# Output projection and two feed-forward pairs read their tokens woven from both halves of the sequence

## The chip, the cores and the metric

The kernel runs on one core of a Trainium2 chip. The metric is the device time of one execution in microseconds; lower is better. A core has a matrix engine (TensorE, PE in the profile), which multiplies a stationary operand of 128x128 (loaded by a separate instruction, PEld) with a moving operand of up to 512 columns and accumulates the product in a bank of PSUM; a vector engine (VectorE, DVE), a scalar engine (ScalarE, ACT) and GpSimd (POOL) for elementwise work; and DMA queues, here those of SyncE (SP) and GpSimd.

## The reference, cut to what matters

One decoder block over 512 tokens, float32, with a model width of 1024 and a feed-forward width of 2816:

```python
h = rmsnorm(x, norm1_g)
proj = h @ w_in                      # short convolution, attention and merge gates
...
mix = gm[..., :D_MODEL] * (y_a @ w_a_out) + gm[..., D_MODEL:] * (y_b @ w_b_out)
x = x + mix @ w_o                    # the output projection
h = rmsnorm(x, norm2_g)
gu = h @ w_ffn_in
g = causal_dwconv(gu[..., :D_FF], ffn_conv_w) + ffn_conv_b
x = x + (silu(g) * gu[..., D_FF:]) @ w_ffn_out
```

## The kernel before, in words

Everything is kept transposed: channels lie on the 128 partitions and the 512 tokens along the free dimension. A float32 product is made of three products in the chip's `float32r` type: each operand is split into a high part (a rounded copy, names ending in `h`) and a low part (the rest, names ending in `l`), and `dense` issues, for each block of 128 inputs, high weight by high x (L158), high weight by low x (L161) and low weight by high x (L163, or L165 where the low weights come in a loop of their own after the others, `lo_last`). The matmuls of one call accumulate in one PSUM region, `acc`.

The stages follow one another on TensorE: input projections, attention, convolution and gates, the output projection, the feed-forward part. A scheduler that simulates the program orders the instructions of each engine; `behind` adds a few orders by hand.

The output projection runs over eight tiles of 128 output channels, in the order 0, 4, 1, 5, 2, 6, 3, 7 (`n` counts the place, `j` the tile). Each loads its weights (`load_w`), takes a bank of 512 columns (tile `po_j`), multiplies the 8 input blocks of `mix_h` and `mix_l` with all 512 tokens, and is added to x by VectorE (L1091). Then `x_forms` makes from it what the feed-forward part multiplies: sums and differences of halves, split again into `xf_h` and `xf_l`, whose last dimension is half the sequence, TH = 256 tokens.

The feed-forward input product goes over pairs of channel tiles, f = 0, 2, ..., 20, each with n = 0 (the convolved gate) and n = 1 (the up part). `ff_pair` makes one n of a pair by Strassen's scheme (in Winograd's form): seven products instead of eight, each by `product`, which accumulates 4 blocks of 128 inputs over 256 columns of half a bank (tile `p`). VectorE combines the halves of the banks (`sums`), and ScalarE copies the first of them (`p1`). The down products (tile `pdn`) of earlier pairs are placed among them by `share`.

Three lines elsewhere are used in the prediction for what they show. L738 and L766 are score products of the attention whose moving operand `kk` is read in two runs; L817 adds a product to an accumulator that it walks as two runs of 128 columns, 256 columns apart (`a4[:, :, b]`). L555 and L566 belong to the compressed keys: L555 multiplies by a row read at every second element, and L566 subtracts operands read at every eighth and every fourth element and writes every fourth. L319 and L199 are plain elementwise lines over contiguous elements.

Of the kernel before, what the change touches and what calls it, by code (L numbers as in the profile page):

```python
# [18 lines left out]
P = 128  # L19
D = 1024  # L20
S = 512
KD = D // P
# [46 lines left out]
HOLD_PT = 4  # L69
HOLD_PO = 6  # L70
A22_BY_DMA = ((0,0),(0,1),)
N_DOWN = 4
N_LAG = 1
INV_FREQ = (10000.0 ** (-np.arange(HALF) / HALF)).astype(np.float32)
# [21 lines left out]
def tile_block(ctx: ExitStack, tc: tile.TileContext, xT, pos, par, par2, w_tok, w_a3, w_gate, w_ao, w_bo, w_o,  # L96
# [12 lines left out]
    def const(shape, name, dt=F32, pool=sb):  # L109
        return pool.tile(shape, dt, name=name, tag=name)  # L110
# [27 lines left out]
    def d_bank(name):  # L138
        return bank("d", name, 2)

    def s_bank(name):
        return bank("s", name, 3)

    def t_bank(name):
        return bank("t", name, 2)

    def o_bank(name):
        return bank("o", name, 1)


    loads, splits = [], []

    def dense(acc, units, first=True, last=True, held={}, lo_last=False):


        n = len(units)
        for i, (wh, wl, xh, xl) in enumerate(units):
            m = nc.tensor.matmul(acc, wh, xh, start=first and i == 0, stop=False)  # L158
            if i in held:
                behind(m, held[i])  # L160
            nc.tensor.matmul(acc, wh, xl, start=False, stop=False)  # L161
            if not lo_last:
                m = nc.tensor.matmul(acc, wl, xh, start=False, stop=last and i == n - 1)  # L163
        for i, (wh, wl, xh, xl) in enumerate(units if lo_last else ()):
            m = nc.tensor.matmul(acc, wl, xh, start=False, stop=last and i == n - 1)  # L165
        return m
# [169 lines left out]
    def behind(later, earlier):  # L336

        tc.add_manual_dep(later.ins, earlier.ins.name,
                          mybir.DependencyInfo(mybir.DependencyClass.NoSync, mybir.DependencyReason.DATA),
                          reason="order")  # L340
# [196 lines left out]
    def w_units(w, xh, xl, nk, k0=0, koff=0):  # L537
        wh, wl = w
        return [(wh[:, (koff + k) * P:(koff + k + 1) * P], wl[:, (koff + k) * P:(koff + k + 1) * P],
                 xh[:, k0 + k, :], xl[:, k0 + k, :]) for k in range(nk)]  # L540
# [453 lines left out]
    def form_a22(f, n, raw, form):  # L994
        h, l = (pw.tile([P, half], F32R, name=f"t{x}{n}_{f}", tag=f"t{x}", bufs=1) for x in "hl")
        if (f, n) in A22_BY_DMA:
            nc.scalar.activation(l, raw[:, half:D], AF.Copy, scale=-1.0)
# [30 lines left out]
    mix_h = const([P, KD, S], "mix_h", F32R, pc)  # L1028
    mix_l = const([P, KD, S], "mix_l", F32R, pc)
    for i in range(4):  # L1030
# [6 lines left out]
        w = load_w(w_bo[i], D, f"bo{i}", after=(ends["pc"], ends["pl"]) if i == 0 else ())  # L1037
        for n, j in enumerate((2 * i, 2 * i + 1)):
            acc = t_bank(f"pmb{j}")
            dense(acc, w_units(w, yb_h, yb_l, 4, koff=4 * n), held={0: gate} if j == 0 else {})  # L1040
            m = tb[j]
# [14 lines left out]
    xf_h = const([P, 4, 7, TH], "xf_h", F32R, px)  # L1056
    xf_l = const([P, 4, 7, TH], "xf_l", F32R, px)
# [5 lines left out]
    def x_forms(j):  # L1063

        k = j % 4
        if j < 4:
            xv[k] = pv.tile([P, 6, TH], F32, name=f"xv{k}", tag="xv", bufs=2)

        v = xv[k]
        o = v[:, 2 * (j // 4):2 * (j // 4) + 2].rearrange("p a t -> p (a t)")  # L1070
        nc.scalar.activation(o, x1[:, j, :], AF.Copy, scale=par_sb[:, G2 + j:G2 + j + 1])
        put = lambda b, a: split(xf_h[:, k, b], xf_l[:, k, b], v[:, a])
        if j < 4:
            nc.vector.tensor_sub(v[:, 4], v[:, 1], v[:, 0])
            put(slice(B11, T1 + 1), slice(0, 5, 4))
        else:
            nc.vector.tensor_sub(v[:, 5], v[:, 3], v[:, 1])
            put(slice(B21, B22 + 1), slice(2, 4))
            nc.vector.tensor_sub(v[:, 0], v[:, 3], v[:, 4])
            nc.vector.tensor_sub(v[:, 1], v[:, 2], v[:, 0])  # L1080
            put(T3, 5)
            put(slice(T2, T4 + 1), slice(0, 2))

    order = [k + 4 * i for k in range(4) for i in range(2)]
    for n, j in enumerate(order):
        w = load_w(w_o[j], D, f"o{j}")
        nc.sync.dma_start(x1[:, j, :], xT[:, j, :])
        acc = d_bank(f"po_{j}")
        dense(acc, w_units(w, mix_h, mix_l, KD), lo_last=True)
        xj = x1[:, j, :]  # L1090
        nc.vector.tensor_add(xj, xj, acc)  # L1091
        x_forms(j)
        sq = sq2 if n == 0 else pc.tile([P, S], F32, name=f"sqb{j}", tag="tb", bufs=3)
        nc.scalar.activation(sq, xj, AF.Square)
        if n > 0:
            nc.vector.tensor_add(sq2, sq2, sq)
# [25 lines left out]
    def ff_pair(f, n, c, form, held=None):  # L1122
        nm = f"{n}_{f}"
        b1, b26 = s_bank(f"p1{nm}"), t_bank(f"p26{nm}")
        b37, b45 = s_bank(f"p37{nm}"), o_bank(f"p45{nm}")
        lo, hi = slice(0, TH), slice(TH, S)

        def product(acc, wf, x, k0=0, k1=4, held={}):
            wh, wl = form[wf]
            dense(acc, [(wh[:, k * P:(k + 1) * P], wl[:, k * P:(k + 1) * P], xf_h[:, k, x], xf_l[:, k, x])  # L1130
                        for k in range(k0, k1)], first=k0 == 0, last=k1 == 4, held=held, lo_last=True)

        def sums(dst, bank, v):

            nc.vector.tensor_tensor(dst, bank.rearrange("p (a t) -> p a t", a=2), v[:, None, :].to_broadcast([P, 2, TH]),
                                    op=ALU.add)

        p1 = pw.tile([P, TH], F32, name=f"p1{nm}", tag="p1", bufs=2)
        c1, c2 = c[:, :, 0:TH], c[:, :, TH:]
        product(b1[:, lo], "a11", B11)  # L1140
        m = nc.scalar.activation(p1, b1[:, lo], AF.Copy)
        if (f, n) == (N_DOWN, 1):
            behind(m, ends["sh"])
        if held:

            product(b45[:, hi], 1, T1)
            product(b26[:, lo], "a12", B21, 0, 3)
            product(b37[:, hi], 3, T3, 0, 3)
            product(b26[:, lo], "a12", B21, 3, 4)
            product(b26[:, hi], 2, T2, held={0: held[0]})  # L1150
            product(b37[:, hi], 3, T3, 3, 4, held={0: held[1]})
        else:
            product(b26[:, lo], "a12", B21)
            product(b26[:, hi], 2, T2)
            product(b37[:, hi], 3, T3)
        sums(c1, b26, p1)
        product(b37[:, lo], 4, B22)
        sums(c2, b37, c1[:, 1])
        if not held:
            product(b45[:, hi], 1, T1)  # L1160
        product(b45[:, lo], "a22", T4)
        sums(c[:, 1].rearrange("p (a t) -> p a t", a=2), b45, c2[:, 1])
        nc.vector.tensor_add(c2[:, 0], c2[:, 0], b45[:, hi])
# [41 lines left out]
    def down_products(f0, n, j0, w, accs=(), last=False):  # L1205

        h, l = w
        per = D // (n * P)
        js = range(j0, j0 + per)
        for j in sorted(js, key=lambda j: last and j not in accs):  # L1210
            cols = [slice(((j - j0) * n + k) * P, ((j - j0) * n + k + 1) * P) for k in range(n)]
            held = j in accs
            for t, acc in accs[j] if held else ((slice(0, S), (d_bank if last or accs == () else t_bank)(f"pdn{j}_{f0}")),):
                acc = acc[:, t]
                dense(acc, [(h[:, c], l[:, c], *(v[:, t] for v in a_hl[f0 + k])) for k, c in enumerate(cols)],
                      first=not (held and last), last=not held or last, lo_last=not accs)
                if held and not last:
                    continue
                xj = x1[:, j, t]
                nc.vector.tensor_add(xj, xj, acc)  # L1220
                if last:
                    (nc.scalar if t.start else nc.sync).dma_start(out[j][:, t], xj)


    def quarter(q):
        return q // N_DOWN * N_DOWN, N_DOWN, D // P // N_DOWN * (q % N_DOWN)

    def share(f, n):
        q = f + n - N_DOWN - N_LAG
        if 0 <= q < NF - N_DOWN - 2:  # L1230
            down_products(*quarter(q), down_weights(*quarter(q), by_dma=True))

    for f in range(0, NF, 2):
# [4 lines left out]
            for j, bank_of in enumerate((d_bank, d_bank, s_bank, s_bank, s_bank, o_bank), 1)}  # L1238
    for n, f0 in ((N_DOWN, NF - N_DOWN - 2), (2, NF - 2)):
        for j in range(0, KD, D // (n * P)):  # L1240
# [66 lines left out]
```

## Time and profile before

| | |
|---|---|
| median of 3 runs | 716.74 us (716.40 to 717.13) |
| span of the profiled execution | 714.1 us |
| TensorE busy | 709.2 us, 99% of the span |
| weight loads busy | 635.9 us, 89% |
| VectorE busy | 573.9 us, 80% |
| ScalarE busy | 414.9 us, 58% |
| granted TensorE clock | 1.000 (mean) |

The span reaches from the first to the last instruction of one profiled execution. The time of that execution with what lies around its span is not recorded apart; the median of the runs is 2.6 us above the span. In the profile, a group of instructions has its line, engine, operation, tiles written and read, shapes and count, then the busy time in us and the mean duration of one in ns, then the idle time of the engine before them. A row of the timeline begins with its start in us and its length in us. A row for one line has the durations (least, median, most) in ns.

### The profile page before, as it was taken

The numbers are of one execution on the slowest core, as the hardware profiler recorded it, in microseconds if no ns is written. First come the engines' busy times: TensorE is split into PE (matmuls) and PEld (weight loads), VectorE is DVE, ScalarE is ACT, GpSimd is POOL, SyncE is SP. The second block draws the span as 40 slices with busy tenths as digits, with TensorE's granted clock in tenths as the row PEclk, the third lists the DMA queues.
The fourth block names the chain that finished last, engine by engine and source line by source line (L and its number), as shares of the span: only waits on it lengthen the run. The fifth ranks groups of instructions, "written<-read, shape, count | busy, mean of one in ns | idle before, by whom it ended". The sixth has DMA issues, their size and how long they took to land.

```text
span 714.1 us, 11190 instructions
## 1 busy us (share of the span) xinstructions
PE 709.2 (99%) x4275; PEld 635.9 (89%) x4275; DVE 573.9 (80%) x988; ACT 414.9 (58%) x706; POOL 124.6 (17%) x111
## 2 busy tenths in 40 slices
PE   9999999999999999999999999999999999999997
PEld 8999888888888888888889999999999999999986
DVE  7978978785566784788876999899898998989833
ACT  7776566777767875444665665555455554455320
POOL 1022443343333311232002011010000010000000
PEclk9999999999999999999999999999999999999999
DMA  8633552121111122246547466745655556552313
GB/s 306 219 86 105 156 127 71 49 90 59 60 60 59 60 63 86 90 146 199 184 133 163 117 149 173 181 119 133 167 144 130 137 127 158 129 148 89 118 30 118
DMA packets 36804, 88.19 MB, mean 124 GB/s; under 512 B 7440, under 2 KB 10896, under 8 KB 36752
## 3 DMA queue, kind: packets, MB, share of 16 engines
q1 hardware_dynamic: 30672, 74.42, 32.7%
q0 software_dynamic: 5648, 12.58, 10.7%
q8 instruction: 33, 0.54, 0.3%
q10 hardware_dynamic: 432, 0.49, 0.2%
q14 instruction: 19, 0.16, 0.1%
HBM read 85.39 MB, written 2.10 MB: 123 GB/s over the span
## 4 chain that ended last, share of the span: by engine, by line
PE 92%; issue 4%; DMA 2%; DVE 1%; POOL 0%; ACT 0%; POOLq 0%; SPq 0%; DVEq 0%
PE p L158 8%; PE p L165 8%; PE p L161 8%; PE pdn L161 4%; PE pdn L158 4%; PE pg L161 4%; PE pg L163 4%; PE pg L158 4%; PE pdn L165 4%; PE pa L158 3%; PE pa L161 3%; PE pt L805 2%; PE po L165 2%; PE po L158 2%; PE po L161 2%
## 5 line engine op out<-in xcount | busy, mean ns | idle before, releaser
L158 PE MATMUL p<-xf_h,sh 128*128 128x256 f32 x352 | 86.4, 280 | 0.0
L161 PE MATMUL p<-xf_l,sh 128*128 128x256 f32 x352 | 86.0, 278 | 0.0
L158 PEld LDWEIGHTS p<-xf_h,sh 128*128 128x128 f32 x352 | 66.5, 189 | 0.1
L161 PEld LDWEIGHTS p<-xf_l,sh 128*128 128x128 f32 x352 | 65.9, 187 | 0.0
L942 ACT ACTIVATE sh<-s 128x1024 fp32r<-128x1024 f32 x44 | 45.7, 1050 | 21.0 <-DVE s L987 17.8
L943 DVE TENSOR_TENSOR sl<-s,sh 128x1024 fp32r<-128x1024 f32 x44 | 53.1, 1215 | 2.8 <-ACT sh L942 2.8
L165 PE MATMUL p<-xf_h,sl 128*128 128x256 f32 x352 | 54.9, 279 | 0.0
L968 POOL DMA_DIRECT2D wl_d<-in_w_dn_dram x16 | 19.1, 1195 | 203.9 <-ACT wl_d L965 203.9
L161 PE MATMUL pdn<-al,wh_d 128*128 128x512 f32 x134 | 52.4, 391 | 0.0
L158 PE MATMUL pdn<-ah,wh_d 128*128 128x512 f32 x134 | 52.0, 390 | 0.0
L163 PE MATMUL pg<-xg_h,wl_g 128*128 128x512 f32 x128 | 50.5, 395 | 0.0
L161 PE MATMUL pg<-xg_l,wh_g 128*128 128x512 f32 x128 | 50.3, 393 | 0.0
L158 PE MATMUL pg<-xg_h,wh_g 128*128 128x512 f32 x128 | 50.3, 393 | 0.0
L165 PEld LDWEIGHTS p<-xf_h,sl 128*128 128x128 f32 x352 | 47.4, 188 | 0.3
L158 PE MATMUL p<-xf_h,wh_s 128*128 128x256 f32 x176 | 43.3, 280 | 0.0
L161 PE MATMUL p<-xf_l,wh_s 128*128 128x256 f32 x176 | 43.1, 278 | 0.0
L756 ACT ACTIVATE e<-sc,mx 128x512 f32<-128x512 f32 (+3 forms) x64 | 33.1, 520 | 16.5 <-DVE mx L755 14.7
L158 PE MATMUL pa<-xg_h,wh_a 128*128 128x512 f32 x96 | 37.9, 395 | 0.0
L161 PE MATMUL pa<-xg_l,wh_a 128*128 128x512 f32 x96 | 37.6, 392 | 0.0
L782 ACT ACTIVATE e<-e,sums 128x512 f32<-128x512 f32 (+3 forms) x64 | 30.7, 552 | 8.2 <-DVE sums L732 8.0
L809 DVE TENSOR_TENSOR pl<-pt,ph 128x512 fp32r<-128x512 f32 x40 | 27.2, 683 | 10.2 <-ACT ph L808 10.0
L165 PE MATMUL pdn<-ah,wl_d 128*128 128x512 f32 x128 | 34.2, 389 | 0.0
(361 smaller groups left out, 2108.9 us busy)
## 6 DMA issues: line engine op xcount, KB each, us to landing
wr_s<-in_w_ff_dram SPq DMA_DIRECT2D x44, 512.0 KB, 3.7
wr_d<-in_w_dn_dram SPq DMA_DIRECT2D x22, 512.0 KB, 3.7
wr_g<-in_w_gate_dram SPq DMA_DIRECT2D x16, 512.0 KB, 3.5
wl_d<-in_w_dn_dram POOLq DMA_DIRECT2D x16, 512.0 KB, 7.0
wr_a<-in_w_a_dram SPq DMA_DIRECT2D x12, 512.0 KB, 3.5
wr_t<-in_w_tok_dram SPq DMA_DIRECT2D x10, 524.0 KB, 5.3
wr_o<-in_w_o_dram SPq DMA_DIRECT2D x8, 512.0 KB, 3.5
wr_ao<-in_w_ao_dram SPq DMA_DIRECT2D x4, 512.0 KB, 3.4
```

What stands on the lines that cost most here:

```text
L158: m = nc.tensor.matmul(acc, wh, xh, start=first and i == 0, stop=False)
L161: nc.tensor.matmul(acc, wh, xl, start=False, stop=False)
L163: m = nc.tensor.matmul(acc, wl, xh, start=False, stop=last and i == n - 1)
L165: m = nc.tensor.matmul(acc, wl, xh, start=False, stop=last and i == n - 1)
L756: nc.scalar.activation(e[:, i, 0:nk], sc[:, o:o + nk], AF.Exp, bias=mx[:, i], accum_out=sums[:, i])
L782: nc.scalar.activation(v, v, AF.Copy, scale=sums[:, i])
L805: ends["pt"] = nc.tensor.transpose(pt[:, i * P:(i + 1) * P], e[:, i, kt * P:(kt + 1) * P], ident)
L809: m = nc.vector.tensor_sub(pl, pt, ph.bitcast(F32))
L942: m = nc.scalar.activation(h, v, AF.Copy)
L943: nc.vector.tensor_sub(l, v, h.bitcast(F32))
L968: nc.gpsimd.dma_start(view(l), src, accum_op=ALU.add)
```

## The change

`woven(t, m)` gives another view of an operand of n columns: the columns are split into two halves (`h`) of n/2 and each half into runs of m columns (`b`), and the view walks run 0 of the first half, run 0 of the second, run 1 of the first, and so on. It is used for the moving operands, high and low, and for the accumulator alike, so every column lands where it did.

In the output projection m goes by the place `n`: the first tile stays as it is, and the others take 128, 64, 32, 16, 8, 4 and 2. In the feed-forward pairs, all products of f = 10 take m = 64 and all of f = 14 take m = 4, for both n; the others stay. Which instructions each engine executes, and in what order and with what waits, is the same in both kernels; the moving and accumulating operands of 168 + 336 matmuls have three dimensions along the partition instead of one (128 x 2 x 2 instead of 512 for the last tile of the projection). The change adds lines to the file: L158, L161 and L165 are L166, L169 and L173 after it.

```diff
+READ_O = (0, 128, 64, 32, 16, 8, 4, 2)
+READ_F = {10: 64, 14: 4}
...
+    def woven(t, m):
+
+        n = t.shape[-1]
+        v = t.rearrange("p (h a b) -> p a h b", h=2, b=m)
+        return v if m > 1 else t.rearrange("p (h a) -> p a h", h=2)
...
         acc = d_bank(f"po_{j}")
-        dense(acc, w_units(w, mix_h, mix_l, KD), lo_last=True)
+        units, m = w_units(w, mix_h, mix_l, KD), READ_O[n]
+        at = (lambda t: woven(t, m)) if m else (lambda t: t)
+        dense(at(acc), [(h, l, at(xh), at(xl)) for h, l, xh, xl in units], lo_last=True)
         xj = x1[:, j, :]
...
             wh, wl = form[wf]
-            dense(acc, [(wh[:, k * P:(k + 1) * P], wl[:, k * P:(k + 1) * P], xf_h[:, k, x], xf_l[:, k, x])
+            at = (lambda t: woven(t, READ_F[f])) if f in READ_F else (lambda t: t)
+            dense(at(acc), [(wh[:, k * P:(k + 1) * P], wl[:, k * P:(k + 1) * P], at(xf_h[:, k, x]), at(xf_l[:, k, x]))
                         for k in range(k0, k1)], first=k0 == 0, last=k1 == 4, held=held, lo_last=True)
```

## The prediction

> **What bounds the kernel now.** I read the page first: its busy shares, slices and chain.
>
> ```profile
> span 714.1 us, 11190 instructions
> ...
> PE 709.2 (99%) x4275; PEld 635.9 (89%) x4275; DVE 573.9 (80%) x988; ACT 414.9 (58%) x706; POOL 124.6 (17%) x111
> ...
> PE   9999999999999999999999999999999999999997
> ...
> PEclk9999999999999999999999999999999999999999
> ...
> PE 92%; issue 4%; DMA 2%; DVE 1%; POOL 0%; ACT 0%; POOLq 0%; SPq 0%; DVEq 0%
> ```
>
> TensorE is busy in every slice, at full granted clock, and carries 92% of the chain. A busy row alone does not prove it the bound, so I ask for the timeline at the places that the change touches: the last tile of the output projection, and the first products of the pair f=10.
>
> ```profile
> 366.98 0.39 PE L158 MATMUL po<-mix_h,wh_o 128*128 128x512 f32 x1
> 367.21 0.39 PE L161 MATMUL po<-mix_l,wh_o 128*128 128x512 f32 x1
> 367.43 0.39 PE L158 MATMUL po<-mix_h,wh_o 128*128 128x512 f32 x1
> 367.66 0.39 PE L161 MATMUL po<-mix_l,wh_o 128*128 128x512 f32 x1
> ...
> 504.99 0.28 PE L158 MATMUL p<-xf_h,wh_s 128*128 128x256 f32 x1
> 505.11 0.28 PE L161 MATMUL p<-xf_l,wh_s 128*128 128x256 f32 x1
> 505.22 0.28 PE L158 MATMUL p<-xf_h,wh_s 128*128 128x256 f32 x1
> 505.34 0.28 PE L161 MATMUL p<-xf_l,wh_s 128*128 128x256 f32 x1
> 505.46 0.28 PE L158 MATMUL p<-xf_h,wh_s 128*128 128x256 f32 x1
> ```
>
> The second column is the time from start to result, and results overlap; what counts is the distance of starts. It is (367.66 - 366.98)/3 = 0.227 us at 512 columns and (505.46 - 504.99)/4 = 0.117 us at 256. The difference, 0.110 us for 256 columns, is 0.43 ns a column; some 7 ns a matmul are fixed. So TensorE streams without holes here, and each nanosecond that a woven stream adds lengthens the kernel.
>
> Each matmul also has a weight load, on a path of its own. Where the matmuls are short, the loads set the pace:
>
> ```profile
> 108.44 0.53 PE L738 MATMUL pcm<-kk,qT 128*128 128x64 f32 x4
> 108.80 0.48 PE L727 MATMUL sc<-kk,qT 128*128 128x512 f32 x1
> ...
> 108.77 0.19 PEld L727 LDWEIGHTS sc<-kk,qT 128*128 128x128 f32 x1
> 108.88 0.19 PEld L728 LDWEIGHTS sc<-kk,qT 128*128 128x128 f32 x1
> ```
>
> Two loads stand 0.11 us apart. At 256 columns the stream (0.117) is only just slower than its load (0.11): a slower stream has no cover there either.
>
> **The change, part by part.** No instruction is added, removed or moved, and each matmul streams as many columns as before. What changes is the walk: m columns of the first half of the operand, m of the second half, the next m of the first, and so on, in the moving operand and in the accumulator alike. Call each change of half a jump. How many matmuls there are comes from the groups by shape:
>
> ```profile
> L158 PE MATMUL po<-mix_h,wh_o 128*128 128x512 f32 x64 | 24.7, 389 | 0.0
> ...
> L158 PE MATMUL p<-xf_h,sh 128*128 128x256 f32 x352 | 86.4, 280 | 0.0
> ...
> L158 PE MATMUL p<-xf_h,wh_s 128*128 128x256 f32 x176 | 43.3, 280 | 0.0
> ...
> L158 PE MATMUL p<-xf_h,th 128*128 128x256 f32 x88 | 21.6, 280 | 0.0
> ```
>
> Each is one of three lines with the same count. The projection has 3 x 64 = 192 matmuls for 8 tiles, 24 a tile; seven tiles are woven, 168 matmuls. The pairs have 3 x (352 + 176 + 88) = 1848 for 11 values of f, 168 each; two are woven, 336 matmuls.
>
> Jumps: a matmul of 512 columns in runs of m makes 512/m - 1. For m = 128 to 2 that is 3 + 7 + 15 + 31 + 63 + 127 + 255 = 501, by 24 matmuls 12,024. The pairs make 3 (m = 64) and 63 (m = 4): 66 x 168 = 11,088. In all 23,112.
>
> *Price of a jump.* The trace has moving operands that are walked in two runs: L738 in runs of 32, L766 in runs of 160 columns; and one accumulator, L817, whose two runs of 128 stand 256 columns apart.
>
> ```profile
> 42.33 0.31 PE L236 MATMUL pj_s<-th,xg_h 128*128 128x320 f32 x1
> 42.48 0.31 PE L239 MATMUL pj_s<-th,xg_l 128*128 128x320 f32 x1
> 42.62 0.31 PE L243 MATMUL pj_s<-tok_lo,xg_h 128*128 128x320 f32 x1
> ...
> 240.79 0.46 PE L766 MATMUL sc<-kk,qT 128*128 128x320 f32 x2
> 241.08 0.27 PE L805 MATMUL pt<-ident,e 128*128 128x128 f32 x1
> ...
> 143.51 0.40 PE L817 MATMUL po<-pc,vc_t 128*128 128x256 f32 x2
> 143.75 0.40 PE L163 MATMUL pa<-xg_h,wl_a 128*128 128x512 f32 x1
> ...
> L817 PE MATMUL po<-pc,vc_t x16: 277/281/287, 143.5 to 286.9; 128*128 128x256 f32 x16
> ```
>
> Contiguous, 320 columns take (42.62 - 42.33)/2 = 0.145 us; with a jump in the moving operand (241.08 - 240.79)/2 = 0.145. With a jump in the accumulator, 256 columns take (143.75 - 143.51)/2 = 0.120 against 0.117, and the median duration of 281 ns is the 280 of the contiguous rows above. Rounded starts leave about 1 ns of doubt. The ends are therefore 0 and 1 ns a jump, 0 to 23 us in all; nothing is saved, since as many columns pass. I take 0, since the rows nearest to the change, those on TensorE itself, show none.
>
> *Price of a run so short that a fetch is half used.* TensorE shows no such walk; VectorE and ScalarE do, while they read and write the same memory.
>
> ```profile
> L319 DVE TENSOR_TENSOR sq_sum<-sq_sum,sq 128x512 f32<-128x512 f32 x7 | 4.8, 685 | 0.4 <-ACT sq L317 0.4
> ...
> L555 DVE TENSOR_TENSOR kc<-kc,rb_n 64x512 f32<-64x512 f32 x4 | 2.7, 686 | 0.9 <-ACT rb_n L447 0.9
> ...
> L566 DVE TENSOR_TENSOR kc<-kc,kc 128x272 fp32r<-128x272 f32 x4 | 2.7, 734 | 0.0
> ...
> L199 DVE TENSOR_TENSOR tok_lo<-wr_t,wh_t 128x1048 fp32r<-128x1048 f32 x4 | 5.0, 1246 | 0.8 <-ACT wh_t L189 0.8
> ...
> L199 DVE TENSOR_TENSOR tok_lo<-wr_t,th 128x320 fp32r<-128x320 f32 x2 | 1.0, 484 | 0.0
> ```
>
> L555 reads one operand at every second element, and takes 686 ns where the contiguous L319 takes 685: using half of what lies side by side is free there. L566 reads every eighth element and writes every fourth. The two L199 rows give VectorE (1246 - 484)/(1048 - 320) = 1.05 ns an element, so 272 contiguous ones would take 434 ns; L566 takes 734, or 2.15 ns an element. Elements two apart evidently share a fetch and elements four apart do not: a fetch looks like four elements (an estimate from these rows). Runs of 4 columns and more then use whole fetches. Only runs of 2, one tile, ask for twice as many. Upper end: TensorE's fetch of four takes the 4 x 0.43 = 1.72 ns that a contiguous stream needs; the 256 runs of a matmul take 440 ns where the stream takes 220, and 24 x 220 ns = 5.3 us are added. Lower end 0, the row L555. I take 0, since a run of 2 is nearer to L555 (two of four used) than to L566 (one of four).
>
> *The accumulators.* The walk there has the same jumps; from L817 I take 0. VectorE evacuates them in the plain order afterwards, as before; weight loads keep their 0.11 us under 0.227 and 0.117.
>
> Sum: 0 + 0 + 0 on the profiled execution's span of 714.1 us. The median of the runs shown, 716.74 us, stands 2.6 us above that span; I carry the 2.6 over and predict 716.8 us.
>
> **The rivals.**
>
> *Runs of 2 cost double.* If TensorE gets no new fetch sooner than every 1.72 ns, the last projection tile takes twice as long: 716.7 + 5.3 = 722.0 us, slower. For it: VectorE's 2.15 ns for a fetch of its own (L566) is longer than the 0.86 ns in which TensorE eats two columns, so L555 proves less for TensorE than for VectorE, whose two elements take 2.1 ns. Against it: no row shows TensorE short of data. It decides from the point where a fetch takes longer than 0.86 ns.
>
> *Each jump costs.* A lost column of 0.43 ns at each of 23,112 jumps gives 9.9 us, 726.6 us. If instead each new place costs the 2.15 ns of L566, runs of 2 take 550 ns a matmul (330 more, by 24: 7.9 us), runs of 4 take 275 in the projection (55 more: 1.3 us) and 138 in the pair f=14 (28 more, by 168: 4.7 us): 13.9 us, 730.6 us. Against it: L766 and L817 have jumps that cost under 1 ns, and 2.15 ns a fetch would starve even the contiguous stream unless that one fetches ahead. 0.43 ns is below what those rows can resolve.
>
> *The accumulators are slow wherever they are not contiguous.* Were the stream halved there, the 168 matmuls would gain 220 ns and the 336 gain 110 ns: 37 + 37 = 74 us, 791 us. L817, with a jump at 128 columns and no cost, speaks against it.
> [...]
>
> *A gain.* Reads that alternate between two places might collide less with the weight loads. At most the fixed 7 ns of the 504 matmuls could go, 3.5 us; half of it gives 715.0 us. No row supports it.
>
> That the walk stays contiguous after all would also give 716.8; the operands of the built kernel are three-dimensional (for the last tile 128 x 2 x 2), so I give it nothing of its own.
>
> **How the numbers follow.** No cost: 0.52; double for runs of 2: 0.24; a cost at each jump: 0.14; slow accumulators: 0.06; a gain: 0.04. The likeliest gives 716.8 us, with a range of its own of 715.9 to 718.2. For eight in ten the range must take in the doubled tile (722.0) and the lower part of the third case: 715.9 to 727. That holds 0.52 + 0.24 and some two thirds of 0.14; the rest is left out. The runs before spread over 0.7 us, so 0.2% (1.4 us) is about what can be told from no change. Faster 0.04, same 0.52, slower 0.24 + 0.14 + 0.06 = 0.44.
>
> **What would show it.** In the changed kernel the starts of the projection's matmuls should stand 0.227 us apart in all eight tiles, eight L173 rows of a tile taking 1.8 us whatever m is, and those of f=10 and f=14 0.117 us. If only the last tile is longer, near 0.44 us a matmul, the first rival holds; if the distance grows with every halving of m and f=14 is longer than f=10, the second; if m = 128 and f=10 are slow already, the third. I would be wrong if jumps too cheap for single-jump rows add up, or if TensorE's fetches are as slow as VectorE's.

## The result, and the profile after

The changed kernel takes 721.26 us (median of 3 runs, 721.13 to 721.95) against 716.74 us: 1.0069 times the time before (95% interval 1.0049 to 1.0089), slower by 4.5 us. The profiled execution is the slowest of the three. Its page, with the span, the busy shares and the shares of the chain by engine:

```profile
span 719.9 us, 11190 instructions
...
PE 714.7 (99%) x4275; PEld 637.8 (89%) x4275; DVE 573.9 (80%) x988; ACT 416.0 (58%) x706; POOL 124.8 (17%) x111
...
PE 91%; issue 4%; DMA 3%; DVE 1%; POOL 0%; ACT 0%; SPq 0%; POOLq 0%; DVEq 0%
```

There are as many instructions as before, VectorE's busy time is the same 573.9 us, and TensorE is busy 5.5 us longer in a span 5.8 us longer. Its waits can have grown by 0.3 us at most: TensorE itself is slower. The timeline of TensorE shows where, in the tiles with m = 16 and m = 2 and the pairs f=10 (m = 64, at 509 us) and f=14 (m = 4, at 570 us). Columns are start and length in us.

```profile
351.09 0.40 PE L169 MATMUL po<-mix_l,wh_o 128*128 128x512 f32 x1
351.33 0.40 PE L166 MATMUL po<-mix_h,wh_o 128*128 128x512 f32 x1
351.57 0.40 PE L169 MATMUL po<-mix_l,wh_o 128*128 128x512 f32 x1
...
368.56 0.49 PE L166 MATMUL po<-mix_h,wh_o 128*128 128x512 f32 x1
368.88 0.50 PE L169 MATMUL po<-mix_l,wh_o 128*128 128x512 f32 x1
369.20 0.50 PE L166 MATMUL po<-mix_h,wh_o 128*128 128x512 f32 x1
369.53 0.50 PE L169 MATMUL po<-mix_l,wh_o 128*128 128x512 f32 x1
...
509.10 0.28 PE L166 MATMUL p<-xf_h,wh_s 128*128 128x256 f32 x1
509.22 0.28 PE L169 MATMUL p<-xf_l,wh_s 128*128 128x256 f32 x1
...
570.17 0.29 PE L166 MATMUL p<-xf_h,wh_s 128*128 128x256 f32 x1
570.29 0.29 PE L169 MATMUL p<-xf_l,wh_s 128*128 128x256 f32 x1
570.42 0.29 PE L166 MATMUL p<-xf_h,wh_s 128*128 128x256 f32 x1
```

Starts stand 0.240 us apart at m = 16, (369.53 - 368.56)/3 = 0.323 at m = 2, 0.12 at f=10 as before, and (570.42 - 570.17)/2 = 0.125 at f=14. From here on, "pace" is the mean distance of starts over all matmuls of a tile or a pair (24 or 168), taken from the trace in ns:

| walk, both sides | contiguous | m = 128 | 64 | 32 | 16 | 8 | 4 | 2 |
|---|---|---|---|---|---|---|---|---|
| projection, 512 columns | 226.7 | 226.7 | 226.7 | 236.7 | 240.0 | 243.1 | 249.8 | 327.8 |
| pairs, 256 columns | 116.7 | | 116.7 | | | | 126.6 | |

The added time: in the last tile 24 x 101.1 ns = 2.4 us; in the tiles from m = 32 to 4, 24 x (10.0 + 13.3 + 16.4 + 23.1) ns = 1.5 us; in f=14, 168 x 9.9 ns = 1.7 us. In all 5.6 us, of the 5.8 by which the two profiled spans differ; the medians differ by 4.5.

### The profile page after: what moved, and what is told of

It reads as the page before. It is cut to its first block, busy times and chain, and to the rows that moved or that the text cites. A ratio compares the mean times of both kernels' runs of the same rounds, so it can differ in the third digit from the quotient of the medians.

```text
span 719.9 us, 11190 instructions
## 1 busy us (share of the span) xinstructions
PE 714.7 (99%) x4275; PEld 637.8 (89%) x4275; DVE 573.9 (80%) x988; ACT 416.0 (58%) x706; POOL 124.8 (17%) x111
## 4 chain that ended last, share of the span: by engine, by line
PE 91%; issue 4%; DMA 3%; DVE 1%; POOL 0%; ACT 0%; SPq 0%; POOLq 0%; DVEq 0%
PE p L173 8%; PE p L166 8%; PE p L169 8%; PE pdn L169 4%; PE pdn L166 4%; PE pg L171 4%; PE pg L169 4%; PE pg L166 4%; PE pdn L173 4%; PE pa L166 3%; PE pa L169 3%; PE pt L813 2%; PE po L173 2%; PE po L169 2%; PE po L166 2%
## 5 line engine op out<-in xcount | busy, mean ns | idle before, releaser
L166 PE MATMUL p<-xf_h,sh 128*128 128x256 f32 x352 | 86.9, 281 | 0.0
L169 PE MATMUL p<-xf_l,sh 128*128 128x256 f32 x352 | 86.7, 279 | 0.0
L166 PEld LDWEIGHTS p<-xf_h,sh 128*128 128x128 f32 x352 | 66.5, 189 | 0.1
L169 PEld LDWEIGHTS p<-xf_l,sh 128*128 128x128 f32 x352 | 65.9, 187 | 0.0
L950 ACT ACTIVATE sh<-s 128x1024 fp32r<-128x1024 f32 x44 | 45.8, 1052 | 21.6 <-DVE s L995 18.4
L173 PE MATMUL p<-xf_h,sl 128*128 128x256 f32 x352 | 55.3, 280 | 0.0
L169 PE MATMUL pdn<-al,wh_d 128*128 128x512 f32 x134 | 52.4, 391 | 0.0
L166 PE MATMUL pdn<-ah,wh_d 128*128 128x512 f32 x134 | 52.0, 390 | 0.0
L169 PE MATMUL pg<-xg_l,wh_g 128*128 128x512 f32 x128 | 50.3, 393 | 0.0
L166 PE MATMUL pg<-xg_h,wh_g 128*128 128x512 f32 x128 | 50.3, 393 | 0.0
L173 PEld LDWEIGHTS p<-xf_h,sl 128*128 128x128 f32 x352 | 47.7, 188 | 0.3
L166 PE MATMUL p<-xf_h,wh_s 128*128 128x256 f32 x176 | 43.6, 281 | 0.0
L169 PE MATMUL p<-xf_l,wh_s 128*128 128x256 f32 x176 | 43.4, 280 | 0.0
L166 PE MATMUL pa<-xg_h,wh_a 128*128 128x512 f32 x96 | 37.9, 395 | 0.0
L169 PE MATMUL pa<-xg_l,wh_a 128*128 128x512 f32 x96 | 37.6, 392 | 0.0
L817 DVE TENSOR_TENSOR pl<-pt,ph 128x512 fp32r<-128x512 f32 x40 | 27.1, 682 | 10.1 <-ACT ph L816 10.0
L173 PE MATMUL pdn<-ah,wl_d 128*128 128x512 f32 x128 | 34.2, 389 | 0.0
```

The source lines that it names most:

```text
L817: m = nc.vector.tensor_sub(pl, pt, ph.bitcast(F32))
L950: m = nc.scalar.activation(h, v, AF.Copy)
```

## The experiments

Unless said otherwise a run is compared with runs of the kernel before on the same chip, and the tiles named are those of the projection in the order of their place. "Moving only" means that accumulators stay contiguous and tokens are not put back.

### Which side pays, and by what

The first four kernels share one edit: `walk` gives a view for a kind ("w" woven as in the change, "s" all even runs and then all odd ones), a size m, and the sides to which it applies (x moving, a accumulator).

```diff
+        if kind == "w":
...
+            return t.rearrange("p (h a b) -> p a h b", h=2, b=m)
+        if kind == "s":
...
+            return t.rearrange("p (a h b) -> p h a b", h=2, b=m)
...
+        at = lambda t, side: walk(t, READ_O[n], side)
+        dense(at(acc, "a"), [(h, l, at(xh, "x"), at(xl, "x")) for h, l, xh, xl in units], lo_last=True)
```

**Moving operands alone** (sizes as in the change, sides "x"):

> The moving operands are walked woven as in the changed kernel (same sizes), the accumulators contiguously; the tokens of the woven tiles therefore land in woven order and are not put back. Theory A, the price is paid where the moving operand is read: the projection's tiles keep the starts of the changed kernel, 0.227 us apart down to runs of 64, then 0.237, 0.240, 0.243, 0.250 and 0.328 for runs of 32, 16, 8, 4 and 2, the pair with runs of 4 keeps 0.127, and the kernel takes 721.3 us. Theory B, it is paid where the accumulator is written: 0.227 and 0.117 everywhere, 716.7 us. Theory C, both walks pay: something between in each tile.

**Accumulators alone** (sides "a"):

> The other half of the change: the accumulators are walked woven, the moving operands contiguously; the tokens land in another order and are not put back. Theory A (reading the moving operand): 0.227 and 0.117 us everywhere, 716.7 us. Theory B (writing the accumulator): 0.328 us in the tile with runs of 2, 0.127 in the pair with runs of 4, 721.3 us. Theory C: what e1 leaves of each tile's excess, so that the two runs add up to it.

The first took 721.63 us, 1.0072 times the time before (1.0052 to 1.0091); the second 716.13 us, 0.9998 times (0.9987 to 1.0008). The timeline in the last tile of the projection, moving operands woven in runs of 2:

```profile
368.41 0.50 PE L180 MATMUL po<-mix_l,wh_o 128*128 128x512 f32 x1
368.74 0.50 PE L177 MATMUL po<-mix_h,wh_o 128*128 128x512 f32 x1
```

The same tile, and the pair f=14 at 566 us, with only the accumulators woven:

```profile
366.67 0.39 PE L177 MATMUL po<-mix_h,wh_o 128*128 128x512 f32 x1
366.90 0.39 PE L180 MATMUL po<-mix_l,wh_o 128*128 128x512 f32 x1
...
565.73 0.28 PE L180 MATMUL p<-xf_l,wh_s 128*128 128x256 f32 x1
565.85 0.28 PE L177 MATMUL p<-xf_h,wh_s 128*128 128x256 f32 x1
```

0.33 us against 0.23: the first has every pace of the changed kernel within 0.2 ns (m = 32 to 2 and f=14), the second 226.7 and 116.7 (227.2 in the tile with m = 4, as in the kernel before). The whole price lies on the reading of the moving operand; an accumulator walked in runs of 128 down to 2 costs nothing here.

**Sizes in another order** (both sides; the projection's places take m = 0, 128, 2, 4, 8, 16, 32, 64, and f = 4 to 14 take 64, 32, 16, 8, 4, 2):

> The whole change, but with the sizes of the projection in another order (contiguous, 128, 2, 4, 8, 16, 32, 64) and with more sizes in the pairs: 64, 32, 16, 8, 4, 2 for f = 4, 6, 8, 10, 12, 14. If the price belongs to the size of the run, the third tile takes 0.328 us a matmul and the last 0.227, and the pairs show 0.117 at 64, at most 0.007 more at 32, 16 and 8, 0.127 at 4 and 0.167 at 2 (half of the projection's excess, half as many columns). If it belongs to the place in the program (what the other engines and the transfers do beside it), the last tiles stay the slow ones.

It took 733.52 us (one run). The timeline in the pair f=14, now with m = 2:

```profile
596.09 0.34 PE L177 MATMUL p<-xf_h,wh_s 128*128 128x256 f32 x1
596.26 0.34 PE L180 MATMUL p<-xf_l,wh_s 128*128 128x256 f32 x1
```

In the projection paces went with the size: 339.2 ns at m = 2, 250.5, 243.3, 240.0, 236.2 and 227.5 at 4 to 64. So the place in the program, or the work beside it, does not set them. In the pairs m = 32, 16, 8, 4 and 2 gave 118.7, 120.2, 123.3, 126.6 and 173.1.

**Every other run** (kind "s", the same sizes as in the change in the projection, 64 to 2 in f = 4 to 14): all even runs and then all odd ones. There are as many jumps as in a woven walk, but the other half of a group of four columns comes only in the second half of the matmul.

> Same sizes as in the changed kernel, and 64 to 2 in the pairs, but another walk on both sides: all even runs of m columns in order, then all odd ones. Each step skips m columns instead of changing between two halves. Theory D, a run shorter than a fetch wastes part of it: the tile with runs of 2 still takes 0.328 us a matmul, since each visit uses half of what lies side by side. Theory E, the two halves 256 columns apart get in each other's way: no such pair of places exists here, and all tiles take 0.227 us. If every jump had a fixed price, the excess would be the same as in the changed kernel in all sizes (0.010 to 0.023 at runs of 32 to 4).

It took 742.13 us (one run). The timeline at m = 4 (362 us) and m = 2 (371 us):

```profile
362.65 0.40 PE L177 MATMUL po<-mix_h,wh_o 128*128 128x512 f32 x1
362.89 0.40 PE L180 MATMUL po<-mix_l,wh_o 128*128 128x512 f32 x1
...
370.93 0.63 PE L180 MATMUL po<-mix_l,wh_o 128*128 128x512 f32 x1
371.38 0.63 PE L177 MATMUL po<-mix_h,wh_o 128*128 128x512 f32 x1
```

Runs of 4 read this way have a pace of 233.1 ns, less than woven (249.8); runs of 2 have 450.4, twice the contiguous pace, where woven ones have 1.45 times. A jump as such has therefore no single price. Neither theory on record came as it stood: D forecast 328 ns at m = 2, and E 227 ns in all tiles, where m = 32 and 16 took 236.3 and 239.7. The doubling of the first rival came where the other half of an aligned four is read in the second half of the matmul (450.4 ns), and not where it is read two columns later (327.8).

### Does the loss add up

All seven tiles in runs of 2, pairs contiguous, with `READ_O = (0, 2, 2, 2, 2, 2, 2, 2)` and `READ_F = {}` in the changed kernel:

> A dose: all seven woven tiles of the projection in runs of 2, the pairs contiguous. If the tile's longer matmuls go to the end of the kernel in full, seven tiles add 7 x 24 x 0.101 to 0.113 us = 17 to 19 us, 733 to 735 us. If other engines or transfers had hidden part of it (that is, if TensorE were not the only bound there), less.

It took 734.74 us, 1.0256 times the time before (1.0239 to 1.0273). The timeline in the third tile:

```profile
345.24 0.51 PE L169 MATMUL po<-mix_l,wh_o 128*128 128x512 f32 x1
345.58 0.51 PE L166 MATMUL po<-mix_h,wh_o 128*128 128x512 f32 x1
```

The seven tiles have paces of 339.6 to 340.0 ns: 7 x 24 x 113.3 ns = 19.0 us, and the medians differ by 18.4. The same walk had 327.8 ns in the last tile of the changed kernel and has 340.0 there now; no run shows why. The loss of a matmul is a loss of the kernel, with no cover: that step of the prediction holds.

### What the reading pays for

Three kernels change moving operands, with H places 512/H columns apart read in turn, m columns from each, and a shift of the whole walk against the groups of four. In the pairs (256 columns) the same form is used, and in three pairs of the second kernel it is put on the accumulators alone (side "a").

```diff
+    def walk(t, places, m):
+        if m == 1:
+            return t.rearrange("p (h a) -> p a h", h=places)
+        return t.rearrange("p (h a b) -> p a h b", h=places, b=m)
...
+        at = k * S + shift - (4 if shift and k == KD - 1 else 0)
+        v = t.rearrange("p k s -> p (k s)")[:, at:at + S]
```

**How many places**, with m = 2 or other small runs:

> Only the moving operands are walked; the accumulators are contiguous, so tokens land in another order, and one tile reads other tokens (the first two of every four columns of two input blocks, in turn). The walk goes over H places, m columns at each, then the next m at each. Projection: m = 2 with H = 128, 64, 16, 4, 2, then the two blocks (two far places, no group of four columns seen twice), then m = 1 with H = 2. Pairs f = 2 to 20: (H, m) = (128, 1), (64, 1), (16, 4), (4, 4), (4, 2), (8, 2), (16, 2), (32, 2), (2, 2), (8, 4). Theory F: a new aligned group of four columns takes the time of four columns, 1.67 ns, however few are used, and a group visited a short while ago is still at hand and costs its columns only. Then H = 128 takes 0.45 us, as many places also 0.45, H = 2 0.33, the two blocks 0.45, m = 1 with H = 2 about 0.39; pairs: 0.229, 0.44 (one column of each group), 0.117 to 0.127 with m = 4, and with m = 2 0.173 for as many places as stay at hand and 0.229 beyond. Theory G: two distant places are served faster in turn than neighbours (three columns' time a visit): the two blocks take 0.33 us, m = 1 with H = 2 0.65, and the rest goes by the distance of the places.

**Where the runs begin**:

> Only the moving operands, with the tokens read from a column that is not a multiple of four (the products are those of shifted tokens, and tokens land in another order). Projection tiles 1 to 7: contiguous, shifted by 2; every other run of 4, shifted by 2; runs of 4 woven from two halves, shifted by 2; every other run of 4, not shifted; every other run of 8, shifted by 2; every other run of 2, shifted by 1; the same shifted by 3. Theory F (aligned groups of four): 0.227; 0.45 (each run touches two groups); 0.33 (one new group and one still at hand); 0.233; 0.33 (three groups for eight columns); 0.45 (still one group a run); 0.87 (two groups a run of 2). Rival, the price goes by the length of the run alone: 0.227, 0.233, 0.250, 0.233, 0.233, 0.450, 0.450. Pairs f = 4 to 10: moving operand with (H, m) = (4, 8), (8, 8), (4, 16), (8, 16), 0.117 to 0.124 us in both. Pairs f = 12, 14, 16: accumulators alone in (64, 2), (2, 2), (32, 4): 0.117 us.

The first took 873.02 us and the second 740.31 us (one run each). The timeline of the first, the pair f=2 read at every second column (445 us) and the last tile, read from two places one column at a time (398 us):

```profile
398.22 0.38 PE L177 MATMUL po<-mix_h,wh_o 128*128 128x512 f32 x1
398.44 0.38 PE L180 MATMUL po<-mix_l,wh_o 128*128 128x512 f32 x1
398.65 0.38 PE L177 MATMUL po<-mix_h,wh_o 128*128 128x512 f32 x1
...
445.37 0.42 PE L177 MATMUL p<-xf_h,wh_s 128*128 128x256 f32 x1
445.60 0.42 PE L180 MATMUL p<-xf_l,wh_s 128*128 128x256 f32 x1
```

The second's timeline, every other run of 4 shifted by 2 columns (345 us) and not shifted (362 us):

```profile
344.72 0.64 PE L180 MATMUL po<-mix_l,wh_o 128*128 128x512 f32 x1
345.18 0.64 PE L177 MATMUL po<-mix_h,wh_o 128*128 128x512 f32 x1
...
361.87 0.40 PE L177 MATMUL po<-mix_h,wh_o 128*128 128x512 f32 x1
362.10 0.40 PE L180 MATMUL po<-mix_l,wh_o 128*128 128x512 f32 x1
```

Three things follow. The same runs of 4 take 456.3 ns shifted and 233.8 unshifted: what counts is the aligned group of four columns (16 bytes), not the run. A walk that changes the group at every column (every fourth column of a pair) takes 233 ns, one that changes it at every second (every second column) takes 229: theory F, by which each change of group costs a fetch, forecast 0.44 us for the first, and falls. Every other run of 2 takes 450 to 453 ns whether it straddles two groups (shift 3) or not. The 0.87 us on record for shift 3 does not follow from F, so it decides nothing: the columns go 3, 4, 7, 8, and 4 and 7 lie in one group, so the group changes at every second column as it does unshifted. And the walk that goes to another place at every single column, with the most jumps of all, is the fastest of the projection: 216.8 ns, 10 below the contiguous 226.7. Theory G forecast 0.65 us for it, and 0.33 for the first two of every four columns of two input blocks in turn, which took 492 ns; G falls too. Runs of 2 read from 4 places or more took 443 ns and more. The three pairs with walked accumulators kept 116.7.

**Two lanes.** The theory L that fits these: the columns of a walk go by turns, odd and even, to two lanes. A lane that comes to another group than its last pays the time of four columns (an estimate, 1.72 ns: four times the 110 ns by which 512 columns take longer than 256, over 256; the texts on record have 1.67), which is hidden if it takes two columns in succession from each group; going back to a group just left costs half (an estimate from the 327.8 ns of woven runs of 2 against 450.4 for every other run of 2). Then four columns of one group in a row are free, two are not, and with one column from each of two places each lane stays in its own place and takes all four of a group. Its rival M: far places are simply read together.

```diff
+        if m < 0:
+            return t.rearrange("p (a h c) -> p a c h", h=2, c=-m)
```

With m = -4 this reads columns 0, 4, 1, 5, 2, 6, 3, 7 and so on; with -2 0, 2, 1, 3; with -8 0, 8, 1, 9; places 4, 8 and 16 with m = 1 go round that many places column by column.

> Only the moving operands are walked; tokens land in another order (and shifted by 2 in the last tile). Projection tiles 1 to 7: one column in turn from 2, 4 and 8 places (H = 2, 4, 8, m = 1); then, in each block of 8 columns, 0 4 1 5 2 6 3 7; in each block of 4, 0 2 1 3; in each block of 16, 0 8 1 9 and so on; then 0 4 1 5 2 6 3 7 shifted by 2 columns. Theory L (two lanes): the columns of a walk go in turn through two lanes, and a lane that changes to another aligned group of four columns than its last takes 1.67 ns for it, or half of that for a group it left a short while ago, unless it takes two columns from the group in succession. H = 2: 0.217 us as before; H = 4: about 0.28; H = 8: 0.28 to 0.45; 0 4 1 5: 0.217, though the two places are neighbours, since each lane takes four columns from one group; 0 2 1 3: 0.227, as contiguous; 0 8 1 9: 0.217; shifted: 0.227. Rival M (memory): two places far apart are read together and near ones are not: H = 2, 4 and 8 0.217, the three walks in small blocks 0.45 us like every other column. Pairs f = 2 to 16: H = 2 with m = 1; 0 4 1 5; 0 2 1 3; H = 4, 8, 16 with m = 1; blocks of 16; blocks of 32: under L 0.110 to 0.115 (no less than a weight load takes), the same, 0.117, 0.145, 0.145 to 0.23, the same, 0.11, 0.11.

It took 760.72 us (one run). Its timeline, eight places column by column (350 us), and the columns 0, 4, 1, 5 (358 us):

```profile
349.78 0.67 PE L179 MATMUL po<-mix_h,wh_o 128*128 128x512 f32 x1
350.27 0.67 PE L182 MATMUL po<-mix_l,wh_o 128*128 128x512 f32 x1
...
358.67 0.38 PE L182 MATMUL po<-mix_l,wh_o 128*128 128x512 f32 x1
358.88 0.38 PE L179 MATMUL po<-mix_h,wh_o 128*128 128x512 f32 x1
359.10 0.38 PE L182 MATMUL po<-mix_l,wh_o 128*128 128x512 f32 x1
```

Neighbouring groups read by turns (0, 4, 1, 5) have the fast pace of two far places, 216.6 ns (median 216), so distance is not what makes it: M falls. Columns 0, 2, 1, 3, in which both lanes stay in one group, have the contiguous 226.8. Shifted by 2, the columns 0, 4, 1, 5 take 227.9, as L forecast. Four places give 283.0 (L: 280), eight 490.0, more than the 450 that L allows; in the pairs 4, 8 and 16 places give 143, 222 and 220, within what it allows. L is a model that fits most of these paces; the lanes themselves appear in no row, and that the contiguous stream is 11 ns slower than the fast walk was put into L's forecasts, not worked out from it.

**Is a jump's small price fixed?** What stayed was the 10 to 23 ns of m = 32 to 4, which L does not explain, since those runs hold whole groups. One kernel takes runs of 4 by turns from two places D columns apart, with equally many jumps everywhere:

```diff
+APART_O = (0, 256, 260, 264, 272, 288, 320, 512)
+APART_F = {2: 128, 4: 132, 6: 136, 8: 144, 10: 160, 12: 192, 14: 256, 16: 130}
...
+        v = flat[:, at:at + 2 * d].rearrange("p (h x) -> p h x", h=2)[:, :, 0:n // 2]
+        return v.rearrange("p h (a b) -> p a h b", b=m)
```

> Only moving operands are walked; accumulators are contiguous and tokens are not put back, so outputs hold other tokens' values and some tokens are read from a neighbouring place. Runs of 4 columns are taken in turn from two places D columns apart: projection tiles 1 to 7 have D = 256, 260, 264, 272, 288, 320, 512 (tile 0 contiguous), the pairs f = 2, 4, 6, 8, 10, 12, 14, 16 have D = 128, 132, 136, 144, 160, 192, 256, 130 (the others contiguous). Jumps are equally many everywhere. If a change of place has one price whatever its distance: about 0.250 us for each matmul of projection tiles 1 to 7 and 0.127 us in the walked pairs. If the small excess comes from where the two places lie to each other (so that reads of two places collide or not): it varies with D, between 0.227 and 0.25 or more in the projection and between 0.115 and 0.134 in the pairs. Two lanes (odd and even columns, a change of the aligned group of four hidden if the lane takes two columns of it in succession) says nothing of D as long as it is a multiple of 4; for D = 130 the second place's runs straddle two groups, so half of its runs cost more: about 0.14 us in that pair against 0.127.

It took 737.79 us (one run). Its timeline in the pairs with D = 144 (485 us), 256 (600 us) and 130 (616 us):

```profile
485.00 0.29 PE L169 MATMUL p<-xf_l,sh 128*128 128x256 f32 x1
485.12 0.29 PE L166 MATMUL p<-xf_h,sh 128*128 128x256 f32 x1
...
600.11 0.29 PE L166 MATMUL p<-xf_h,sh 128*128 128x256 f32 x1
600.24 0.29 PE L169 MATMUL p<-xf_l,sh 128*128 128x256 f32 x1
...
615.70 0.34 PE L169 MATMUL p<-xf_l,sh 128*128 128x256 f32 x1
615.87 0.34 PE L166 MATMUL p<-xf_h,sh 128*128 128x256 f32 x1
```

| D modulo 64 | 0 | 4 | 8 | 16 and 32 |
|---|---|---|---|---|
| pairs (116.7 contiguous) | 126.6 to 126.8 | 126.9 | 123.6 | 120.1, 120.0 |
| projection (226.7 contiguous) | 250.0 to 250.6 (D = 256, 320, 512) | 253.5 | 243.0 | 241.0, 240.2 |

The price is not fixed for a jump. In the distances tried it goes with their remainder modulo 64 columns (256 bytes), largest at 0 and 4, smallest at 16 and 32; what makes the remainder count no run shows. Within this the change's halves, 256 and 128 columns apart, lie in the first column of the table, among the dearest. Pairs of the kernel that tried the number of places agree with the table's order: runs of 4 took 134 ns from 4 places 64 columns apart, 124 from 8 places 32 apart, and 115, less than contiguous, from 16 places 16 apart. At D = 130, where the second place's runs straddle two groups, the pace is 172.8 ns against the 140 that L forecast: the half price for going back to a group is not general. If those returns are charged in full, L gives 1.5 x 116.7 = 175.

### A version that beats both

The fast walk in the kernel before: moving operands of the gates, convolution, merges, output projection, pairs and down products are read from the two halves one column at a time, and the VectorE and ScalarE instructions that evacuate each accumulator write the tokens back to their places.

```diff
+    def walk(t):
+        return t.rearrange("p (h a) -> p a h", h=2)
+    def back(t):
+        return t.rearrange("p (a h) -> p h a", h=2)
...
-            dense(acc, [(wh[:, k * P:(k + 1) * P], wl[:, k * P:(k + 1) * P], xf_h[:, k, x], xf_l[:, k, x])
+            dense(acc, [(wh[:, k * P:(k + 1) * P], wl[:, k * P:(k + 1) * P], walk(xf_h[:, k, x]), walk(xf_l[:, k, x]))
...
-        nc.vector.tensor_add(xj, xj, acc)
+        nc.vector.tensor_add(tok(xj), tok(xj), back(acc))
```

> The kernel before, but with the moving operands of the gates, the convolution, both merges, the output projection, the feed-forward pairs and the down products walked column by column from two places in turn (H = 2, m = 1), and with VectorE and ScalarE putting the tokens back in order as they empty the contiguous accumulators. If each matmul of 512 columns saves the 10 ns seen at H = 2 and one of 256 the 2 to 6 ns down to its weight load: 1566 x 10 ns + 1848 x 2 to 6 ns = 19 to 27 us, 690 to 697 us. Rival: emptying an accumulator at every second column costs VectorE up to twice (a row of 685 ns becomes 1.2 us, some 180 of them: 100 us of VectorE on its 574), TensorE then waits for banks, and the gain goes down to nothing or below.

It took 692.28 us (4 runs, 691.23 to 693.04), 0.9672 times the time before (0.9656 to 0.9688). Its page, its timeline in the projection (352 us) and the first pair (361 us), and the one new group of TensorE whose wait is above 0.3 us:

```profile
PE 682.8 (99%) x4275; PEld 628.8 (91%) x4275; DVE 570.8 (83%) x988; ACT 412.0 (60%) x706; POOL 124.0 (18%) x111
...
PE 86%; DMA 5%; issue 5%; DVE 2%; ACT 1%; POOL 1%; DVEq 0%; POOLq 0%; SPq 0%; ACTq 0%
```

```profile
352.02 0.38 PE L170 MATMUL po<-mix_h,wh_o 128*128 128x512 f32 x1
352.23 0.38 PE L173 MATMUL po<-mix_l,wh_o 128*128 128x512 f32 x1
...
360.87 0.28 PE L170 MATMUL p<-xf_h,wh_s 128*128 128x256 f32 x1
360.98 0.28 PE L173 MATMUL p<-xf_l,wh_s 128*128 128x256 f32 x1
```

```profile
L177 PE MATMUL p<-xf_h,wl_s 128*128 128x256 f32 x176 | 28.1, 279 | 2.1 <-DMA wl_s<-in_w_ff_dram 2.1
```

The pace is a median of 216 ns at 512 columns (1566 matmuls so read) and a median of 112 at 256 (1848). The gain worked out from these is 1566 x 10.7 + 1848 x 4.7 ns = 25.4 us; 23.5 us arrived, and the wait for weights of 2.1 us is about as long as the difference. VectorE pays nothing for the stride (570.8 us busy against 573.9; an addition of a down product to x takes a mean of 683 ns against 680).

## Why the prediction was right or wrong, point by point

- **The time**: 716.8 us was forecast, from no cost at all (chance 0.52), and that case did not come. The 721.26 us lie within the range of 715.9 to 727 because the range took in two rivals, neither of which came as it stood.
- **TensorE is the bound, and each added nanosecond lengthens the kernel**: right. 19.0 us put into seven tiles came out as 18.4.
- **Nothing added, removed or moved; accumulators 0**: right. Accumulators alone: 0.9998 (0.9987 to 1.0008). With it falls the third rival, the slow accumulators: no run shows the halved stream of its 791 us, and with the accumulators woven the matmuls kept 226.7 ns at 512 columns and 116.7 at 256.
- **Price of a jump, 0 of 0 to 23 us**: mis-sized. It measured 3.2 us, 1.5 in the tiles m = 32 to 4 and 1.7 in f=14. The rows L766 and L817 could not show it: a jump or two in a matmul at 0.2 to 0.7 ns each is lost in starts rounded to 10 ns, which over two matmuls leave some 5 ns of doubt and not the 1 ns written there. And the price is not one for a jump: 23 ns at m = 4 (127 jumps) but 10 ns at m = 32 (15 jumps), and between 3.3 and 10 ns at equal jumps in the pairs as the distance of the places changes. The second rival took a fixed price, a column (9.9 us) or a VectorE fetch (13.9 us), and fails in both sizes and in form.
- **Half-used fetches, 0 of 0 to 5.3 us**: the step that failed. It measured 24 x 101 ns = 2.4 us, with whatever the 255 jumps of that tile cost, near the middle of its bounds. I took 0 because two of four used is free on VectorE (L555, 686 ns against 685). On TensorE two of four cost double, 450 ns at 512 columns, when the other two come much later. Weaving brings the other two back two columns later, and then a matmul takes 1.45 to 1.5 times the contiguous pace (327.8 to 340.0 ns against 226.7). The first rival named the right tile; its doubling of runs of 2 came with every other run read (450.4 ns) and not with the woven walk, and it missed that the longer runs pay too (236.7 to 249.8 ns at m = 32 to 4). That its 722.0 us lies near 721.26 is thus partly an accident: 2.4 us instead of its 5.3, with 3.2 us that it did not have.
- **The fetch of four elements, an estimate from L555, L566 and L199**: right for TensorE too, as to its size: with every other aligned run of 4 a matmul takes 233 ns, 1.03 times the contiguous 226.7, and shifted by 2 it takes 456, twice that. That a fetch lies behind it is an estimate; no row shows one.
- **A gain, at most the fixed 7 ns of a matmul**: not in this change, whose walks were all equal or slower. But reading by turns from two places did save 11 ns at 512 columns once m was 1, and the 7 ns did not limit it. The same split of the fast walk's 215.8 and 111.6 ns leaves 7 ns fixed and 0.41 ns a column: the saving lies in the columns, whose 0.43 ns the prediction took as given, unless the weight loads, 0.11 us apart, hold up the shorter matmuls.
- **What would show it**: starts 0.227 and 0.117 us apart everywhere did not come, nor 0.44 in the last tile alone. The distance grew with every halving below 64, and f=14 was longer than f=10, as I had written for the second rival.

The median difference is 4.5 us, and the paces give 5.6; the spans of the three runs are 719.2 to 719.9, 5.1 to 5.8 above the one profiled span of before. The rest of the difference is within the spread of the runs.

What stays open is why places 64 columns apart, or a multiple of it, cost most, why eight places by turns take 490 ns, when a return to a group is cheap (woven runs of 2 took 327.8 ns against 450.4), why the contiguous stream is slower than two places column by column, and why runs of 2 take 328 ns in some tiles and 340 in others.

## What to carry to other kernels

Where TensorE is the bound, look at how its moving operand lies. Here a walk in runs that kept aligned groups of four `float32r` columns together took 227 to 254 ns at 512 columns from one or two places (226.7 contiguous); runs of 2 took 328 to 492, every other run of 4 shifted by 2 took 456, and a stride of 2 took 229 in a pair (116.7 contiguous). The accumulator could be walked in any of the orders tried here (runs of 2 and more) for nothing: 226.7 and 116.7 ns as before. If the evacuation can put columns back at no cost, try reading two places column by column: here it took 4.7% off each 512-column matmul and 3.3% off the kernel. A price read from VectorE, or from a row with one jump, was here an end of a range for TensorE, not its middle.

## What the runs showed of the hardware that was not expected

- A contiguous `float32r` stream is not the fastest: 226.7 ns at 512 columns against 215.8 for one column from each of two places, and 117 against 112 at 256.
- Two columns in a row of an aligned group of four were not enough to keep the contiguous pace of 226.7 ns: aligned runs of 2 took 450 ns when every other run was read. Four in a row nearly kept it (233 ns for every other aligned run of 4), and two walks whose every second column stays in one group were faster: 216.8 ns for one column in turn from two places, 216.6 for the columns 0, 4, 1, 5.
- A contiguous operand that begins 2 columns off a group of four took about 233 ns in its tile of the shifted run, instead of 226.7.
